# Five query projections in seven products, and smaller moves around them, in a two-layer decoder trunk

## The chip, the cores and the metric

One core of one Trainium2 chip runs the whole kernel. The metric is the device time of one execution in microseconds (us), as the median of several runs. Lower is better. Everything is single precision.

## The reference, cut to what matters

The program is a small decoder trunk. 16 learned rows are put ahead of 512 tokens, so that 528 rows of width 1024 pass through two layers; each layer is a pre-norm branch added to the residual, and a final norm drops the 16 rows. Layer 0 is gated linear attention with 4 heads. Layer 1 is differential attention with 8 heads, and the change is mostly there:

```python
def diff_branch(xn, w_in, lam_vecs, gnorm, w_out, rel_table, lambda_init):
    proj = xn @ w_in                                  # 1024 -> 4 x 2048
    q, k, v, z = jnp.split(proj, 4, axis=-1)
    lam = jnp.exp(jnp.sum(lv[0] * lv[1])) - jnp.exp(jnp.sum(lv[2] * lv[3])) + lambda_init
    ...
    def block(args):                                  # 128 query rows
        s = jnp.einsum('bhpqd,bhpkd->bhpqk', qb, kh) * scale + bias[None, :, None]
        s = jnp.where(dist >= 0, s, -jnp.inf)
        p = jax.nn.softmax(s, axis=-1)                # two maps, p = 0 and 1
        a = p[:, :, 0] - lam * p[:, :, 1]
        return jnp.einsum('bhqk,bhkv->bhqv', a, vh)
    ...
    o = head_rms(o) * gnorm * (1.0 - lambda_init)
    y = jax.nn.silu(z) * o.reshape(B, L, D_INNER)
    return y @ w_out
```

Each head has two query maps and two key maps of width 128, values of width 256 and a gate z of width 256. So q, k, v and z of one head are each a product of the 528 (or the 512 real) normed rows with a 1024 x 256 piece of the weights.

## The kernel before, in words

**Numbers in two parts.** TensorE multiplies float32r operands. To keep precision every operand is split into a high part (a rounded copy, made by ScalarE) and a low part (the difference, made by VectorE) by `split` (L270), and each product is three matmuls: high by high, high by low, low by high. So every weight piece costs one ScalarE and one VectorE instruction before TensorE can use it.

**Two ways to project.** `project` (L414) is the plain one: 8 row blocks of the weights (128 x 128) by three matmuls, 24 matmuls for 128 output columns. For a head's q it runs twice with 512 tokens as the moving operand: 48 matmuls of 512 columns. Its weights come in two parts ("pair"), each a 128 x 1024 split; its result is split straight out of PSUM (L279/L280). A `Unit` (L436) is the other one: the 1024 x 256 piece is cut into 2 x 2 blocks and the rows into two halves of 256 or 264, and seven block products take the place of eight. Each is 12 matmuls (`PASSES`, L42; `product`, L428) of 256 columns where only real tokens are wanted, or of 264. A Unit asks VectorE for four additions of weight blocks (L366), three single splits (a11, a12, a22) and two pair splits (s21, s43); ScalarE copies sums out of PSUM (`partial`, L450, tile u), and four VectorE instructions (L477/L479) put the outputs together. `want_unit` (L356) prepares the weights in the order a11, sums, s21, a12, s43, a22, as far as buffers are free (two pairs, one of each single).

**Units in a chain.** A Unit that is followed by another in the work queue issues the first product of its successor inside its own run (`nxt.first()`, L534), and the successor starts "early". The seven products are p1 to p7 in the code. p1, p6 and p7 gather in one bank of PSUM, bx: after p6 ScalarE copies it (u2), after p7 once more (u3). For an early Unit with no successor, here called lone, the order is p6, p5, p7, p2, p4, p3. Its p7 adds to the bank that u2 is copied from.

**Order of the work.** TensorE's order is the program's order, written out by `Weaver` (L74): a queue of projection work ("filler"), from which `W.fill(us)` issues as much as is asked for, while the attention steps of the current head are put between. VectorE, ScalarE and GpSimd are ordered at build time by priority (`urgent`, `soon`, `at_once`). In layer 1 the loop over heads (L1848) queues, in head hd, the output projection of an earlier pair (`q_diff_out2`, from head 2 on), then z, v, k (Units) and q (plain) of head hd+1. In head 6 the order is k, q, v, z. The key projection may not begin until all scores of the current head are done (`W.stop`, L1868).

**A head's steps** (`diff_steps`, L1675) are A, B, C and E for four blocks of 128 query rows, the longest block (3) first:

- A `scores`: for each map six or twelve matmuls, a VectorE instruction that adds the bias and finds the row's minimum (L1692), an Exp on ScalarE with its sum (L1694). Then VectorE forms the ratio lam x sum0 / sum1 by a reciprocal (L1697) and a small product (L1698), and combines the two maps (L1699).
- B `turn`: transposes of the combined map, and a split (L1707 to L1713).
- C `values`: product with v, a row norm with a power on GpSimd (L1730).
- E `rows`: two transposes of the result (L1737), product with the gate (L1740), and a split.

The list at L1882 gives the order. After each step `W.fill` gets a share of the filler that is left:

```python
        share = {A: 1.5, B: 1.1, C: 1.1, E: 0.5}
        ...
        W.fill(3.0)
        ...
            W.fill(max((W.left - keep) * share[f] / sum(share[g] for g, _ in steps[n:]),
                       ((4.0, 3.0, 5.2, 3.0, 4.6, 3.0, 4.0, 3.0)[hd]) if n == len(steps) - 2 else 2.4 if f is C else 0.0))
```

The last head runs the first six steps so, and the rest in a sequence written out at the end of the kernel, between the parts of the last output projection (L1916 on).

Of the kernel before, what the change touches and what calls it, by code (L numbers as in the profile page):

```python
# [11 lines left out]
F32 = mybir.dt.float32  # L12
# [197 lines left out]
def trunk(ctx, tc, x, meta, g_norm, gla_w_in, gla_w_gate_up, gla_b_gate, gla_gnorm, gla_w_out,  # L210
# [225 lines left out]
    class Unit:  # L436
# [188 lines left out]
    dve.memset(mhalf, -0.5)  # L625
    warm = ps_tile()
# [1035 lines left out]
    def q_diff_q(hd, s):  # L1662
        want_diff(256 * hd)

        def gen():
            for i in range(2):
                bank = pb_tile("bx" if hd else ("bv", "by")[i])
                yield from project(ws.take(), real2, None, NR, [by_halves(bank)])
                assert not hd or heads[hd - 1].scored
                if i == 0:  # L1670
                    s.q = [T(ep, [P, 2, NR], F32R, f"q{j}", bufs=1) for j in range(2)]
                urgent(split)(*[t[:, i, :] for t in s.q], bank, scale=-float(P) ** -0.5)
        return W.add(gen(), 10.3)

    def diff_steps(hd, s, ys):  # L1675
# [3 lines left out]
        def scores(b):  # L1679
# [4 lines left out]
            r.p = []  # L1684
            ko = L - nk
            for m in range(2):
# [8 lines left out]
                r.p.append(p[:, :nk])  # L1695

            dve.reciprocal(st[:, 5:6], st[:, 3:4])  # L1697
            dve.scalar_tensor_tensor(st[:, 5:6], st[:, 5:6], lam, st[:, 2:3], op0=ALU.mult, op1=ALU.mult)  # L1698
# [35 lines left out]
        def rows(r):  # L1734
            pt = ps_tile()
            for m in range(2):
                pe.transpose(pt[:, m * P:(m + 1) * P], r.on[:, m * P:(m + 1) * P], ident)  # L1737
            y = T(ep, [P, 2, P], F32, "yt")
            cs = slice(r.ta, r.ta + P)
            W.mark = dve.tensor_tensor(y, pt[:, :256].rearrange("p (m c) -> p m c", m=2), s.z[:, :, cs], op=ALU.mult)  # L1740
# [7 lines left out]
        return A, lambda b: turn(R[b]), lambda b: values(R[b]), lambda b: rows(R[b])  # L1748
# [99 lines left out]
    for hd in range(D_HEADS):  # L1848
# [24 lines left out]
        if hd == D_HEADS - 2:  # L1873
# [3 lines left out]
            def freed():  # L1877
# [4 lines left out]
        steps = [(A, 0), (A, 1), (B, 0), (A, 2), (C, 0), (B, 1), (E, 0), (A, 3), (C, 1), (B, 2), (E, 1), (C, 2), (B, 3),  # L1882
                 (E, 2), (C, 3), (E, 3)]
# [4 lines left out]
        W.fill(3.0)  # L1888
        for n, (f, b) in enumerate(steps):
# [79 lines left out]
```

## Time and profile before

| what | value |
|---|---|
| median of 3 runs | 971.44 us (970.47 to 972.05) |
| the profiled execution | 970.65 us, its span on the core 968.9 us |
| TensorE clock granted | 0.999 of full speed |
| matmuls | 6993, each with its own weight load |
| VectorE, ScalarE, GpSimd instructions | 1586, 1304, 68 |
| DMA | 104.94 MB, 108 GB/s on average |

In the profile PE is TensorE's matmuls, PEld its weight loads, DVE VectorE, ACT ScalarE, POOL GpSimd, SP the engine that issues most DMAs. A line such as L431 is a line of the kernel; L431 is the matmul of a Unit's products, L421 that of the plain projection, L400 that of everything with both operands in two parts (scores, values, output projection). Matmuls are pipelined, so the shown length of one includes its drain; what one costs in a stream is read from one start to the next.

### The profile page before, as it was taken

Reading aid. Unit: us, or ns where it says so; the run is one execution under the profiler, and the core shown is the slowest. Engines: PE = TensorE matmul, PEld = TensorE weight load, DVE = VectorE, ACT = ScalarE, POOL = GpSimd, SP = SyncE. Lnnn points to the kernel's source line nnn. Section 1 sums busy time; section 2 is a strip of 40 time slices with the busy share of each in tenths; the row PEclk is TensorE's granted clock in tenths of the full one; section 3 lists DMA queues with packets and bytes.
Section 4 is the critical chain, followed back from the end, with each engine's and each line's share of the span. In section 5 each row is a group of like instructions: output and inputs, shape, how many; then the busy total and the mean of one; then the engine's idle time right before and its main releaser. Section 6 shows DMA issues by size and latency. Waiting matters only on the chain.

```text
span 968.9 us, 18048 instructions
## 1 busy us (share of the span) xinstructions
PE 957.2 (99%) x6993; PEld 906.9 (94%) x6993; DVE 778.6 (80%) x1586; ACT 626.8 (65%) x1304; POOL 44.9 (5%) x68
## 2 busy tenths in 40 slices
PE   9999999999999999999999999999999999999997
PEld 8999999999999999998899998998999989989996
DVE  7989885886888787668997987968869769687785
ACT  7776755577647567656757776575675756755583
POOL 1000000000000000000001001000000000000001
PEclk9999999999999999999999999999999999999999
DMA  7322223635363236124355525243342341722212
GB/s 197 88 85 59 82 79 122 147 103 128 116 162 91 85 117 158 53 101 152 99 130 138 143 73 133 75 139 98 99 138 88 118 119 44 182 70 84 89 64 87
DMA packets 128522, 104.94 MB, mean 108 GB/s; under 512 B 51102, under 2 KB 112830, under 8 KB 128433
## 3 DMA queue, kind: packets, MB, share of 16 engines
q1 hardware_dynamic: 123104, 93.80, 35.1%
q10 hardware_dynamic: 5328, 9.95, 2.8%
q8 instruction: 56, 0.92, 0.4%
q14 instruction: 34, 0.27, 0.1%
HBM read 83.64 MB, written 11.80 MB: 99 GB/s over the span
## 4 chain that ended last, share of the span: by engine, by line
PE 88%; ACT 1%; DVE 1%; issue 1%; POOLq 0%; DVEq 0%
PE bx L431 19%; PE bv L431 12%; PE by L431 10%; PE bx L421 10%; PE ps L400 9%; PE bx L972 5%; PE bx L400 3%; PE bv L972 2%; PE by L972 2%; PE ps L1214 2%; PE by L400 2%; PE bv L400 2%; PE ps L1807 1%; PE bx L1807 1%; PE bv L421 1%; PE by L421 1%
## 5 line engine op out<-in xcount | busy, mean ns | idle before, releaser
L277 DVE TENSOR_TENSOR wl<-raw,wh 128x1024 fp32r<-128x1024 f32 x98 | 119.4, 1221 | 23.0 <-ACT wh L276 18.9
L276 ACT ACTIVATE wh<-raw 128x1024 fp32r<-128x1024 f32 x98 | 103.1, 1054 | 48.3 <-PE by L972 22.9
L431 PE MATMUL bv<-x,wh 128*128 128x264 f32 (+1 forms) x656 | 98.6, 287 | 0.0
L431 PE MATMUL bx<-x,wh 128*128 128x264 f32 (+1 forms) x640 | 95.6, 286 | 0.0
L431 PEld LDWEIGHTS bv<-x,wh 128*128 128x128 f32 x656 | 86.8, 189 | 0.6 <-DVE z L479 0.2
L431 PEld LDWEIGHTS bx<-x,wh 128*128 128x128 f32 x640 | 84.6, 188 | 0.7 <-ACT u L452 0.2
L452 ACT ACTIVATE u<-bx 128x264 f32<-128x264 f32 (+1 forms) x120 | 45.3, 379 | 35.5 <-PE bx L431 33.1
L1694 ACT ACTIVATE p<-p,st 128x528 f32<-128x528 f32 (+3 forms) x64 | 36.5, 570 | 41.7 <-DVE st L1692 41.4
L421 PE MATMUL bx<-x,wh 128*128 128x512 f32 (+1 forms) x256 | 62.4, 385 | 0.0
L277 DVE TENSOR_TENSOR wl<-sum,wh 128x1024 fp32r<-128x1024 f32 x41 | 50.1, 1221 | 10.6 <-ACT wh L276 10.5
L431 PE MATMUL bx<-x,wl 128*128 128x264 f32 (+1 forms) x320 | 54.1, 284 | 0.0
L431 PE MATMUL bv<-x,wl 128*128 128x264 f32 (+1 forms) x328 | 53.8, 284 | 0.1
L421 PEld LDWEIGHTS bx<-x,wh 128*128 128x128 f32 x256 | 44.4, 188 | 7.8
L276 ACT ACTIVATE wh<-sum 128x1024 fp32r<-128x1024 f32 x41 | 43.1, 1051 | 9.7 <-PE by L972 3.9
L431 PE MATMUL by<-x,a12h 128*128 128x264 f32 (+1 forms) x320 | 47.5, 286 | 0.1
L1730 POOL TENSOR_TENSOR st<-st,mhalf 128x1 f32<-128x1 f32 x32 | 25.5, 795 | 468.6 <-ACT on L1728 418.2
L431 PE MATMUL bx<-x,a11h 128*128 128x264 f32 (+1 forms) x320 | 46.6, 284 | 0.0
L431 PEld LDWEIGHTS bv<-x,wl 128*128 128x128 f32 x328 | 45.4, 188 | 0.3 <-issue 0.3
L431 PEld LDWEIGHTS bx<-x,wl 128*128 128x128 f32 x320 | 45.3, 188 | 0.3
L431 PEld LDWEIGHTS bx<-x,a11h 128*128 128x128 f32 x320 | 42.4, 188 | 0.6
L431 PEld LDWEIGHTS by<-x,a12h 128*128 128x128 f32 x320 | 42.1, 188 | 0.3 <-ACT t L1658 0.3
L276 ACT ACTIVATE a11h<-raw 128x512 fp32r<-128x512 f32 x41 | 25.7, 626 | 20.7 <-DMA raw<-in_diff_w_in_dram 7.9
(493 smaller groups left out, 2631.9 us busy)
## 6 DMA issues: line engine op xcount, KB each, us to landing
raw<-in_gla_w_in_dram SPq DMA_DIRECT2D x48, 512.0 KB, 4.5
raw<-in_diff_w_in_dram SPq DMA_DIRECT2D x42, 512.0 KB, 4.9
raw<-in_diff_w_in_dram SPq DMA_DIRECT2D x11, 1024.0 KB, 5.9
raw<-in_gla_w_out_dram SPq DMA_DIRECT2D x8, 1024.0 KB, 5.8
raw<-in_diff_w_out_dram SPq DMA_DIRECT2D x8, 1024.0 KB, 6.0
vd<-planes ACTq DMA_DIRECT2D x12, 268.0 KB, 5.8
vd<-keep ACTq DMA_DIRECT2D x12, 264.0 KB, 2.3
T<-bdr SPq DMA_DIRECT2D x8, 264.0 KB, 4.7
```

Source lines behind the costliest of these rows:

```text
L276: act.activation(hi, src, AF.Copy)
L277: dve.tensor_tensor(lo, src, hi.bitcast(F32), op=ALU.subtract)
L400: pe.matmul(ps, l, r, start=first and n == 0, stop=last and n == 2, **kw)
L421: pe.matmul(bank, a[:, k, :], b[k] if n0 is None else b[k][:, n0 + i * nn:n0 + (i + 1) * nn], start=n == 0 and ks[0] == 0, stop=n == len(t ...
L431: pe.matmul(bank[:, :x[q].shape[2]], w[p][:, k * P:(k + 1) * P], x[q][:, k, :], start=first and i == 0, stop=i == len(PASSES) - 1, skip_gr ...
L452: W.moved = act.activation(t, self.bx[:, :self.n], AF.Copy, scale=self.sc)
L972: pe.matmul(banks[i][:, :HT], h.t[p][:, k, mm * P:(mm + 1) * P], s.y[q][k][:, i * HT:(i + 1) * HT], start=n == 0, stop=n == len(PASSES) - 1)
L1214: pe.matmul(o, s.kd[:, i, kc], s.qs[:, i, t0:t0 + n], start=i == 0, stop=i == 1)
L1694: act.activation(p[:, :nk], p[:, :nk], AF.Exp, scale=-1.0, bias=st[:, m:m + 1], accum_out=st[:, 2 + m:3 + m])
L1730: pool.tensor_tensor(ms, ms, mhalf[:, :1], op=ALU.pow)
L1807: pe.matmul(ps[i], yp[hd][p][:, k, b * P:(b + 1) * P], wt[q][cs.start // 512][:, 2 * hd + k, cs.start % 512:(cs.stop - 1) % 512 + 1], star ...
```

## The change

- `q_diff_q`: q of heads 3 to 7 is made by a `Unit` on the 512 real tokens; its two output tiles are then split with the scale already in them. Heads 0, 1 and 2 keep the plain projection. q thereby joins the chain of Units: it follows k early, and in head 6 v follows it.
- A lone Unit writes p7 into a second bank of bx, and the new `third` lets VectorE add u2 to it, where ScalarE copied the sum before.
- The ratio of the two sums is made by three GpSimd instructions; the map with index 1 is scored before the map with index 0.
- `rows` takes two blocks at once (except in the last head): four transposes into one bank, one product with the gate, one split. Two E steps fall out of the list, and yt has one buffer.
- The first fill of a head is 4.0 instead of 3.0; B has at least 2.4 of filler behind it and E at least 1.0.

```diff
+        @at_once
+        def third(self, bank):
+            t = T(up[0], [P, HT], F32, "u", bufs=3)[:, :self.n]
+            if self.sc == 1.0:
+                dve.tensor_tensor(t, bank[:, :self.n], self.u2, op=ALU.add)
+            else:
+                dve.scalar_tensor_tensor(t, bank[:, :self.n], self.sc, self.u2, op0=ALU.mult, op1=ALU.add)
+            return t
...
             def p7():
-                yield from product(self.bx, ws.use(s43)[1], X["t3"], False)
-                self.u3 = self.partial()
+                if early and not nxt:
+                    bank = pb_tile("bx")
+                    yield from product(bank, ws.use(s43)[1], X["t3"])
+                    self.u3 = self.third(bank)
+                else:
+                    yield from product(self.bx, ws.use(s43)[1], X["t3"], False)
+                    self.u3 = self.partial()
                 add(1, 1, self.bv, self.u3, -1)
...
     def q_diff_q(hd, s):
+        scale, qts = -float(P) ** -0.5, []
+
+        def tiles():
+            assert not hd or heads[hd - 1].scored
+            s.q = [T(ep, [P, 2, NR], F32R, f"q{j}", bufs=1) for j in range(2)]
+
+        if hd in (3, 4, 5, 6, 7):
+            def dst():
+                tiles()
+                qts.extend([tok_tile()[:, :NR], tok_tile()[:, :NR]])
+                return qts
+
+            @soon
+            def tail(i):
+                split(*[t[:, i, :] for t in s.q], qts[i])
+
+            return W.add(Unit(want_unit(d_w_in, 256 * hd), Xr, scale, dst, tail), 8.9)
...
-            for m in range(2):
+            for m in (1, 0):
...
-            dve.reciprocal(st[:, 5:6], st[:, 3:4])
-            dve.scalar_tensor_tensor(st[:, 5:6], st[:, 5:6], lam, st[:, 2:3], op0=ALU.mult, op1=ALU.mult)
+            pool.tensor_tensor(st[:, 5:6], st[:, 3:4], minus, op=ALU.pow)
+            pool.tensor_tensor(st[:, 4:5], st[:, 2:3], lam, op=ALU.mult)
+            pool.tensor_tensor(st[:, 5:6], st[:, 5:6], st[:, 4:5], op=ALU.mult)
             dve.scalar_tensor_tensor(r.p[0], r.p[1], st[:, 5:6], r.p[0], op0=ALU.mult, op1=ALU.subtract)
...
         @urgent
-        def rows(r):
+        def rows(*rs):
+            w = P * len(rs)
             pt = ps_tile()
             for m in range(2):
-                pe.transpose(pt[:, m * P:(m + 1) * P], r.on[:, m * P:(m + 1) * P], ident)
-            y = T(ep, [P, 2, P], F32, "yt")
-            cs = slice(r.ta, r.ta + P)
-            W.mark = dve.tensor_tensor(y, pt[:, :256].rearrange("p (m c) -> p m c", m=2), s.z[:, :, cs], op=ALU.mult)
+                for j, r in enumerate(rs):
+                    pe.transpose(pt[:, m * w + j * P:m * w + (j + 1) * P], r.on[:, m * P:(m + 1) * P], ident)
+            y = T(ep, [P, 2, w], F32, "yt", bufs=1)
+            cs = slice(rs[0].ta, rs[0].ta + w)
+            W.mark = dve.tensor_tensor(y, pt[:, :2 * w].rearrange("p (m c) -> p m c", m=2), s.z[:, :, cs], op=ALU.mult)
...
-        steps = [(A, 0), (A, 1), (B, 0), (A, 2), (C, 0), (B, 1), (E, 0), (A, 3), (C, 1), (B, 2), (E, 1), (C, 2), (B, 3),
-                 (E, 2), (C, 3), (E, 3)]
+        steps = [(A, 0), (A, 1), (B, 0), (A, 2), (C, 0), (B, 1), (A, 3), (C, 1), (B, 2), (E, 1), (C, 2), (B, 3),
+                 (C, 3), (E, 3)]
...
-        W.fill(3.0)
+        W.fill(4.0)
...
-                       ((4.0, 3.0, 5.2, 3.0, 4.6, 3.0, 4.0, 3.0)[hd]) if n == len(steps) - 2 else 2.4 if f is C else 0.0))
+                       ((4.0, 3.0, 5.2, 3.0, 4.6, 3.0, 4.0, 3.0)[hd]) if n == len(steps) - 2 else {A: 0.0, B: 2.4, C: 2.4, E: 1.0}[f]))
```

More of the change, by code (lines that the diff above doesn't have):

```diff
@@ L625, in trunk @@
     dve.memset(mhalf, -0.5)
+    minus = cp.tile([P, 1], F32, name="minus")
+    dve.memset(minus, -1.0)
     warm = ps_tile()
@@ L1668, in gen @@
                 yield from project(ws.take(), real2, None, NR, [by_halves(bank)])
-                assert not hd or heads[hd - 1].scored
                 if i == 0:
-                    s.q = [T(ep, [P, 2, NR], F32R, f"q{j}", bufs=1) for j in range(2)]
-                urgent(split)(*[t[:, i, :] for t in s.q], bank, scale=-float(P) ** -0.5)
+                    tiles()
+                urgent(split)(*[t[:, i, :] for t in s.q], bank, scale=scale)
         return W.add(gen(), 10.3)
@@ L1683, in scores @@
             r.st = st = T(ep, [P, 8], F32, "st", bufs=4)
-            r.p = []
+            r.p = [None, None]
             ko = L - nk
-            for m in range(2):
+            for m in (1, 0):
                 p = T(ep, [P, L], F32, "p", bufs=3)
@@ L1746, in A @@
             R[b] = scores(b)
-        return A, lambda b: turn(R[b]), lambda b: values(R[b]), lambda b: rows(R[b])
+        return A, lambda b: turn(R[b]), lambda b: values(R[b]), lambda b: rows(*([R[b]] if hd == D_HEADS - 1 else [R[b], R[b + 1]]))
     def want_last(hd):
```

2 lines of the change are left out of this document (1 added, 1 removed).

## The prediction

> **What bounds the kernel now.** I read the busy times first, then the list of waits with TensorE as the one that waits, then one middle head stretch by stretch, and at last the starts of single matmuls.
>
> ```profile
> PE 957.2 (99%) x6993; PEld 906.9 (94%) x6993; DVE 778.6 (80%) x1586; ACT 626.8 (65%) x1304; POOL 44.9 (5%) x68
> ```
>
> A busy PE need not be a PE at its peak, so this alone settles nothing. The waits do: these are the three longest in total in which TensorE waited for another engine, over 968.9 us.
>
> ```profile
> PE ps L631 <- DVE ones L622: 1.2, 1, 1.2
> PE bx L421 <- DVE wl L277: 0.7, 1, 0.7
> PE ps L1244 <- DVE vm L412: 0.7, 1, 0.7
> ```
>
> None is in a Unit's products (L431), and none above 1.2 us anywhere. TensorE is handed work without a break, and the time is the sum of what its matmuls cost. The windows show the stretches of a middle head (columns: length, then busy PE, PEld, DVE, ACT, POOL): first z, v and k of the next head as Units, then its q by the plain projection, then an output projection with the first scores. The fourth row is a whole head period of 63 us.
>
> ```profile
> 740.30:777.70 37.40, 37.40 (x314) 37.32 (x313) 29.52 (x65) 26.18 (x62) 2.60 (x3) 1.00 0.34 107
> 777.70:789.80 12.10, 12.10 (x59) 9.84 (x58) 6.93 (x14) 6.86 (x15) 0.55 (x1) 1.00 0.61 142
> 789.80:803.50 13.70, 13.70 (x68) 11.61 (x67) 12.41 (x29) 7.07 (x13) 0.00 (x0) 1.00 0.26 78
> ```
>
> ```profile
> 770.00:833.00 63.00, 63.00 (x435) 58.60 (x434) 50.20 (x109) 40.53 (x93) 2.61 (x4) 1.00 0.38 108
> ```
>
> PE fills every one of them at full clock. VectorE has room in the q stretch (6.93 of 12.10 us) and little at the start of a head (12.41 of 13.70, or 91%). So matmul time taken away shortens the run, as long as VectorE still delivers.
>
> **The query projections, matmul side.** What a matmul costs is read from start to start. Here are two products of 256 columns (12 matmuls each, eight by the high and four by the low part), and then a chain of 512-column matmuls of the plain projection (columns: start, length with drain, instruction, count).
>
> ```profile
> 745.89 1.10 PE L431 MATMUL bv<-x,wh 128*128 128x256 f32 x8
> 746.83 0.64 PE L431 MATMUL bv<-x,wl 128*128 128x256 f32 x4
> 747.31 1.10 PE L431 MATMUL bx<-x,wh 128*128 128x256 f32 x8
> 748.25 0.65 PE L431 MATMUL bx<-x,wl 128*128 128x256 f32 x4
> 748.73 0.52 PE L431 MATMUL bx<-x,a11h 128*128 128x264 f32 x3
> ```
>
> ```profile
> 479.08 5.61 PE by L421 x24
> 484.68 5.86 PE bx L421 x48
> ```
>
> From 745.89 to 747.31 and on to 748.73 a product takes 1.42 us, 118 ns for each matmul. From 479.08 to 484.68 the 24 matmuls take 5.60 us, 233 ns for each. One head's q costs 48 x 233 ns = 11.2 us now and seven products of 1.42 us, 9.94 us, after the change. That is 1.23 us less for each head (taking 232.7 ns, since the next inserted step hides a little of the last matmul), and 5 x 1.23 = 6.15 us for heads 3 to 7. It lies wholly on the path, because there PE is the path. Here a page speaks against the change. The Trainium skill, "TensorE: Matmul & The Clock Gate", section Back-to-back issue gap, gives sustained spacings of about 81 ns at 128 columns and 131 ns at 512; by an estimate between its two figures 84 short matmuls would take 8.2 us and 48 long ones 6.3 us, so the seven products would lose. The trace does not agree: its 512-column spacing is 233 ns, and it halves with the columns.
>
> **The same, VectorE's side.** The groups of instructions give the prices (last columns: busy us, mean ns of one, idle before).
>
> ```profile
> L277 DVE TENSOR_TENSOR wl<-raw,wh 128x1024 fp32r<-128x1024 f32 x98 | 119.4, 1221 | 23.0 <-ACT wh L276 18.9 <-PE bx L421 2.9 <-ACT vm L408 0.7
> ...
> L277 DVE TENSOR_TENSOR a11l<-raw,a11h 128x512 fp32r<-128x512 f32 x41 | 28.1, 686 | 12.4 <-ACT a11h L276 12.2
> L366 DVE TENSOR_TENSOR sum<-raw 128x512 f32<-128x512 f32 x41 | 28.1, 686 | 7.0 <-DMA raw<-in_gla_w_in_dram 4.1 <-DMA raw<-in_diff_w_in_dram 2.6
> ...
> L479 DVE TENSOR_TENSOR t<-bv,u 128x264 f32<-128x264 f32 (+1 forms) x33 | 14.0, 425 | 2.9 <-PE bv L431 2.9
> ...
> L1740 DVE TENSOR_TENSOR yt<-ps,z 128x256 f32<-128x256 f32 x32 | 13.4, 418 | 9.6 <-PE ps L1737 9.6
> ...
> L280 DVE SCALAR_TENSOR_TENSOR q<-bx,q 128x512 fp32r<-128x512 f32 x14 | 9.6, 684 | 0.3 <-ACT q L279 0.3
> ...
> L1698 DVE SCALAR_TENSOR_TENSOR st<-st,lam 128x1 f32<-128x1 f32 x32 | 6.9, 216 | 0.6
> ...
> L1697 DVE RECIPROCAL st<-st 128x1 f32<-128x1 f32 x32 | 5.1, 158 | 9.4 <-ACT p L1694 9.4
> ```
>
> The plain q asks VectorE for two pair splits and two result splits: 2 x 1.221 + 2 x 0.684 = 3.81 us. The Unit asks for four block additions, three single splits, two pair splits, four output instructions and two result splits: 4 x 0.686 + 3 x 0.686 + 2 x 1.221 + 4 x 0.425 + 2 x 0.684 = 10.31 us. That is 6.50 us more for each head, at most, since neighbours overlap by some tens of ns. ScalarE gets the same three single splits and two or three bank copies; at 65% busy it has the room. I cost both at nothing as long as they hide under the matmuls. From 740.30 to 789.80 VectorE is busy 29.52 + 6.93 = 36.45 of 49.50 us. The new sum stays below the 48.3 us that PE then needs, even with all of it put there (43.0 us).
>
> **The third product of a lone Unit.** The sum after p7 moves from ScalarE to VectorE, at 425 ns by the row of its like (L479), and p7 no longer waits for the copy of u2. No such wait is among TensorE's waits above, so nothing is gained where it is made now (k of most heads); below nothing it can hardly go, since one VectorE instruction takes the place of one on ScalarE, and both are ahead of the same next one. In the heads that change, the lone Unit is q instead of k: 0.43 us more for VectorE. I take 0 for the time. Without cover, each use would cost its 0.43 us.
>
> **The ratio on GpSimd, and the order of the maps.** Off VectorE go 0.158 + 0.216 us for each block, 1.50 us for each head of four blocks. On GpSimd come three instructions; two of them follow the second sum, since the power needs only the map that is now first. The nearest row is the power of the row norm:
>
> ```profile
> L1730 POOL TENSOR_TENSOR st<-st,mhalf 128x1 f32<-128x1 f32 x32 | 25.5, 795 | 468.6 <-ACT on L1728 418.2 <-DVE wl L277 30.1 <-DVE p L1699 13.2
> ```
>
> So two instructions cost between 0.32 us (if as quick as VectorE's 158 ns) and 1.59 us, against 0.37 us now: the combination of the maps (L1699) comes -0.05 to +1.22 us later. I take +1.2, the like row. L1699 waits in VectorE's queue, and a weight split of 1.22 us may stand behind it, which a Unit waits for; but a split made that much later is still ahead of its product while VectorE has a tenth of its time free. The one who needs the combined map is step B. It has the least room in the last head:
>
> ```profile
> 915.92 0.77 DVE L1699 SCALAR_TENSOR_TENSOR p<-p,st,p 128x528 f32<-128x528 f32 x1
> ```
>
> ```profile
> 919.80 0.60 PE L1707 MATMUL ps<-ident,p 128*128 128x128 f32 x4
> ```
>
> Ready at 916.69, used at 919.80: 3.1 us of cover for 1.2. The time is unchanged. Without that cover it would be 1.2 us for each of 32 blocks. GpSimd's only other work there is the power of step C, which could queue behind a ratio for the same 1.2 us; the filler behind C covers it.
>
> **Rows in pairs, and the fills.** Four transposes stay four transposes for TensorE: no gain. VectorE's four products of 256 columns at 0.418 us and as many split halves of that size become two and two of 512 at 0.684 us (the L280 row): 3.34 us become 2.74, 0.60 less a head. The first block of a pair waits for the second, and its reader is an output projection of a later head. The fills move PE work about and add none. The first one does not even move it where output projections are the filler: they come in steps of 1.4 us (L1784), and 3.0 and 4.0 both take three steps. Cost 0.
>
> **The sum.** TensorE: -6.15 us. VectorE for each changed head: +6.50 + 0.43 - 1.50 - 0.60 = +4.83, so 55.0 of 61.8 us, 89% where it is 80% now. I add 0.2 us of new waits for each of the five heads, 1.0 us in all, taken from the lower part of the first rival's span. The profiled execution took 970.65 us (its span 968.9), 0.8 under the median of 971.44. It should become 965.5, and the median 971.44 - 6.15 + 1.0 = **966.3 us**.
>
> **The rivals.** First, and on the other side: q comes late to the first scores. The rows show q's end before, at the same place of this head.
>
> ```profile
> 789.77 0.40 PE L400 MATMUL bx<-wh,y 128*128 128x512 f32 x1
> ...
> 793.99 1.61 PE L400 MATMUL ps<-k,q 128*128 128x264 f32 x12
> ```
>
> ```profile
> 792.70 0.58 ACT L279 ACTIVATE q<-bx 128x512 fp32r<-128x512 f32 x1
> ...
> 793.67 0.68 DVE L280 SCALAR_TENSOR_TENSOR q<-bx,q 128x512 fp32r<-128x512 f32 x1
> ```
>
> The last matmul of q ends at about 789.77; its ScalarE half starts only at 792.70, 2.9 us later, behind other work, and the low half is done at 794.35, 4.6 us after the end. The scores begin at 793.99, and those of the second map half of 1.46 us later, at 794.72: 0.4 us of room. Afterwards the chain has one VectorE instruction more (an output sum of 0.43 us), at a lower priority. What speaks for room is that the map that is ready first (its outputs are finished one product, 1.42 us, earlier) is scored first, so that the late one has 4.95 us. If the chain grows by 0.43 to 5.0 us, the wait is nothing to 0.1; with one more place in a queue (1.22 us) it is 1.3 us. Up to 0.6 us a head the result stays below 969.5; between 0.9 and 1.23 us for each head nearly all is eaten, about 970 to 971.4. It decides at 1.23 us. If two links of the chain each wait the 2.9 us seen here, the chain is 2 x 2.9 + 0.43 + 0.58 + 0.68 = 7.5 us and the wait 2.5 us a head: 5 x (2.5 - 1.23) = 6.4 us lost, 978 us.
>
> Second: VectorE's new work isn't hidden because it comes in one place. q's pair s43 can be split only when k has given back its own pair, at k's end; q's p7 follows two products (2.84 us) after that. In these come the block addition, the pair split, two output sums and the splits of k: 0.69 + 1.22 + 0.85 + 1.37 = 4.13 us. What is over, 1.3 us, less the time of the first eight matmuls of p7, 0.94 us, is 0.35 us for each head: 967.0 us, with 1.75 us of waits where the sum has 1.0. Against it stands that k is in the same place behind v now, and none of TensorE's waits lies there.
>
> Third: the loads of the weights set the pace, not the columns.
>
> ```profile
> L431 PEld LDWEIGHTS bv<-x,wh 128*128 128x128 f32 x656 | 86.8, 189 | 0.6 <-DVE z L479 0.2
> ```
>
> If each of 84 loads cost its 189 ns, q would take 15.9 us instead of 11.2, +4.7 a head, 995 us. The 118 ns spacing in a stretch where PEld is as full as PE (37.32 of 37.40) says that loads overlap. This is also the way in which the page's spacings above would have it.
>
> Fourth: the change does not do what it says, for a Unit that is not chained (then nothing of the third product applies) or a bank that is not free. The second is the nearer one: p7 takes the second bx, which the Unit before has left long ago. Price 0, and the sum stays.
>
> **How the numbers follow.** About 0.2%, 2 us, is what a measurement of this kernel can tell from no change. Chances: the sum as forecast, waits under 0.6 us a head, with the second rival's size among them, 0.68; the first rival with 0.6 to 1.23 us, 0.17, of which a third is still faster by 2 us; its slower form, 0.11; weight loads, 0.01; a shift elsewhere that returns the gain, 0.03. So faster 0.74, within 0.2% 0.14, slower 0.12. The range reaches from all of the 6.15 us and the waits of today that might go (two of 0.7 us), with the spread of the runs below, 963.1, to the end of the first rival where all is eaten, 971.5; that leaves out its slower form and little else.
>
> **What would show it.** Right: L421 falls by 240 matmuls and L431 rises by 420; a head period of about 61.8 us; VectorE near 89% in a middle head; no wait of TensorE above 0.5 us in heads 2 to 6. Wrong in the first way: waits of scores (L400, ps<-k,q) on the q tile at a head's start. In the second: waits of L431 on the pair split. In the third: starts of q's products more than 130 ns apart. A gain well over 7 us would mean that TensorE's stream had gaps that its waits don't show.

## The result, and the profile after

| | before | after |
|---|---|---|
| median, same chip | 971.19 us (6 runs, 970.47 to 972.05) | 977.01 us (6 runs, 976.63 to 978.37) |
| ratio, 95% interval | | 1.0061 [1.0049, 1.0073]: 0.6% slower |
| profiled execution, its span | 970.65, 968.9 us | 976.72, 974.9 us |

Predicted were 966.3 us. The page's busy times, by engine:

```profile
PE 954.6 (98%) x7173; PEld 912.2 (94%) x7173; DVE 799.6 (82%) x1561; ACT 633.1 (65%) x1309; POOL 83.0 (9%) x164
```

TensorE has 180 matmuls more (240 long ones gone, 420 short ones come), as it should, and they cost what was forecast. A product of q and the start of the next, in the timeline of TensorE:

```profile
722.87 1.10 PE L431 MATMUL bx<-x,wh 128*128 128x256 f32 x8
723.81 0.65 PE L431 MATMUL bx<-x,wl 128*128 128x256 f32 x4
724.29 1.11 PE L431 MATMUL by<-x,a12h 128*128 128x256 f32 x8
```

From 722.87 to 724.29 it is 1.42 us again. So the matmul side gave its 6.15 us. The span grew by 974.9 - 968.9 = 6.0 us all the same, which means that about 12.1 us of waiting came in. The list of TensorE's waits holds 8.4 us of it: it comes to 12.7 us in all, where it came to 4.3 before. It counts a wait only from the end that the profile gives the matmul before it. Read from one start to the next, with the drain of that matmul, the listed places lose 10.6 us more than before, and gaps too short for the list lose the rest (each spacing taken against the median of its shape in the kernel before). From the list (engine and line waited for: us in total, times, longest):

```profile
PE bx L431 <- ACT u L452: 3.7, 4, 1.4
PE ps L1260 <- ACT vm L408: 1.4, 1, 1.4
...
PE by L431 <- DVE t L486: 0.7, 2, 0.3
```

The first line is new: a Unit's product waits until ScalarE has copied the bank that it adds to. The wait at L1260, in the first layer, was 0.7 us before. Of the others about half are new, on ScalarE and VectorE, and none of the new ones is longer than 0.6 us.

Three head periods of the kernel after, from the first scores of one head to those of the next (length, then busy PE, PEld, DVE, ACT, POOL):

```profile
669.28:733.16 63.88, 62.68 (x472) 59.97 (x471) 55.99 (x113) 42.65 (x96) 7.63 (x16) 1.00 0.36 107
733.16:795.50 62.34, 62.17 (x472) 59.86 (x471) 53.22 (x106) 41.95 (x95) 7.75 (x16) 1.00 0.37 109
795.50:859.18 63.68, 62.24 (x471) 59.87 (x470) 54.41 (x109) 42.09 (x95) 7.22 (x16) 1.00 0.38 109
```

The middle one is nearly the forecast 61.8 us. The others are 1.5 and 1.3 us longer, with VectorE busy for 88% and 85% of the time, where the middle one has 85% too. So a share of busy time doesn't tell where it is lost; the places do. ScalarE and TensorE around 809 us:

```profile
808.53 1.06 ACT L276 ACTIVATE wh<-raw 128x1024 fp32r<-128x1024 f32 x1 [1.24 <-DVE raw L366]
809.49 0.37 ACT L452 ACTIVATE u<-bx 128x256 f32<-128x256 f32 x1
```

```profile
809.91 0.97 PE L431 MATMUL bx<-x,wh 128*128 128x256 f32 x6 [1.44 <-ACT u L452]
```

The copy takes 0.37 us and its bank was long full, but ScalarE works in order: a weight split stands ahead of it, and that one waits 1.24 us for a block addition on VectorE. At 911 us it is a split that waits for a DMA:

```profile
910.34 0.63 ACT L276 ACTIVATE a11h<-raw 128x512 fp32r<-128x512 f32 x1 [4.70 <-DMA raw<-in_diff_w_in_dram]
910.88 0.37 ACT L452 ACTIVATE u<-bx 128x264 f32<-128x264 f32 x1
```

```profile
911.30 1.24 PE L431 MATMUL bx<-x,wh 128*128 128x264 f32 x8 [1.35 <-ACT u L452]
```

The Trainium skill, "TensorE: Matmul & The Clock Gate", table of specifications, calls the queues of ScalarE, VectorE and GpSimd strictly first in, first out; these rows of ScalarE agree.

### The profile page after: what moved, and what is told of

It is laid out like the page before. It is cut to its first block, busy times and chain, and to the rows that moved or that the text cites. A ratio compares the mean times of both kernels' runs of the same rounds, so it can differ in the third digit from the quotient of the medians.

```text
span 974.9 us, 18485 instructions
## 1 busy us (share of the span) xinstructions
PE 954.6 (98%) x7173; PEld 912.2 (94%) x7173; DVE 799.6 (82%) x1561; ACT 633.1 (65%) x1309; POOL 83.0 (9%) x164
## 4 chain that ended last, share of the span: by engine, by line
PE 73%; DVE 7%; ACT 5%; DMA 3%; issue 2%; POOL 1%; SPq 0%; POOLq 0%; ACTq 0%; DVEq 0%
PE bx L431 18%; PE bv L431 10%; PE by L431 10%; PE ps L400 7%; PE bx L988 5%; PE bx L421 4%; DMA raw<-in_diff_w_in_dram 3%; PE by L988 2%; PE bv L988 2%; PE ps L1230 2%; PE bx L400 2%; DVE wl L277 1%; ACT p L1726 1%; PE ps L1842 1%; PE bx L1842 1%
## 5 line engine op out<-in xcount | busy, mean ns | idle before, releaser
L431 PE MATMUL bv<-x,wh 128*128 128x264 f32 (+1 forms) x736 | 109.5, 286 | 0.2
L431 PE MATMUL bx<-x,wh 128*128 128x264 f32 (+1 forms) x720 | 105.7, 285 | 3.7 <-ACT u L452 3.7
L431 PEld LDWEIGHTS bx<-x,wh 128*128 128x128 f32 x720 | 94.4, 188 | 5.1 <-ACT u L452 4.7
L431 PEld LDWEIGHTS bv<-x,wh 128*128 128x128 f32 x736 | 96.8, 188 | 1.0 <-DVE t L486 0.3
L277 DVE TENSOR_TENSOR wl<-sum,wh 128x1024 fp32r<-128x1024 f32 x46 | 56.2, 1222 | 12.2 <-ACT wh L276 12.0
L431 PE MATMUL bv<-x,wl 128*128 128x264 f32 (+1 forms) x368 | 61.2, 285 | 0.1
L431 PE MATMUL bx<-x,a11h 128*128 128x264 f32 (+1 forms) x360 | 53.8, 285 | 0.0
L277 DVE TENSOR_TENSOR a11l<-raw,a11h 128x512 fp32r<-128x512 f32 x46 | 31.6, 687 | 17.2 <-ACT a11h L276 17.0
L1729 POOL TENSOR_TENSOR st<-st,minus 128x1 f32<-128x1 f32 x32 | 20.9, 653 | 283.7 <-ACT p L1726 231.5
L556 POOL TENSOR_TENSOR st<-st,mhalf 128x1 f32<-128x1 f32 (+1 forms) x20 | 11.8, 588 | 388.6 <-DVE st L555 388.6
```

What stands on the lines that cost most here:

```text
L277: dve.tensor_tensor(lo, src, hi.bitcast(F32), op=ALU.subtract)
L431: pe.matmul(bank[:, :x[q].shape[2]], w[p][:, k * P:(k + 1) * P], x[q][:, k, :], start=first and i == 0, stop=i == len(PASSES) - 1, skip_gr ...
L556: pool.tensor_tensor(dst, dst, mhalf[:np_, :dst.shape[1]], op=ALU.pow)
L1729: pool.tensor_tensor(st[:, 5:6], st[:, 3:4], minus, op=ALU.pow)
```

## The experiments

Every time below is a median, beside the kernel before on the same chip (970.4 to 970.6 us), with the ratio's 95% interval.

| run | kernel | us | ratio |
|---|---|---|---|
| e1_only_q | before, q of heads 3 to 7 as Units | 970.29 | 0.9998 [0.9989, 1.0007] |
| e2_no_q | after, all q plain | 975.01 | 1.0044 [1.0031, 1.0058] |
| e3_no_third | after, without `third` | 973.36 | 1.0031 [1.0019, 1.0043] |
| e4_ratio_dve | after, ratio on VectorE | 972.12 | 1.0016 [1.0007, 1.0025] |
| e5_no_third_ratio_dve | both of these | 968.80 | 0.9984 [0.9975, 0.9993] |
| e6_third_alone | before, `third` | 974.00 | 1.0031 [1.0019, 1.0044] |
| e7_ratio_alone | before, GpSimd ratio and map order | 974.08 | 1.0036 [1.0023, 1.0048] |
| e8_pairs_fills_alone | before, rows in pairs and fills | 973.38 | 1.0028 [1.0017, 1.0039] |
| e9_ratio_unhurried | e7, combination out of the urgent step | 974.81 | 1.0045 [1.0032, 1.0058] |
| e10_e5_q3to6 | e5, q of head 7 plain | 968.52 | 0.9983 [0.9974, 0.9992] |
| e11_q3to6_order | before, q of heads 3 to 6, map order | 970.15 | 0.9993 [0.9984, 1.0001] |
| e12_q3to6_order_pairs | e11, rows in pairs | 974.34 | 1.0035 [1.0020, 1.0049] |
| e13_order_alone | before, map order | 971.47 | 1.0013 [1.0005, 1.0022] |
| e15_ratio_behind_copy | e7, Exp behind the copy of u | 970.94 | 1.0004 [0.9995, 1.0013] |
| e16_q3to6_ratio_behind_copy | e18, ratio on GpSimd | 971.80 | 1.0013 [1.0004, 1.0022] |
| e17_third_second_layer | before, `third` in the second layer | 972.38 | 1.0024 [1.0013, 1.0035] |
| e18_q3to6_behind_copy | e10, Exp behind the copy of u | 967.94 | 0.9973 [0.9963, 0.9983] |
| e19_fills_alone | before, fills | 973.59 | 1.0036 [1.0023, 1.0050] |

**The query Units against the rest.** Theory A: the q Units themselves bring the waits, through the copies of u on ScalarE. Theory B: the parts beside q do. e1 puts only the new `q_diff_q` into the kernel before, e2 takes only that out of the kernel after:

```diff
-        if hd in (3, 4, 5, 6, 7):
+        if hd in ():
```

> Kernel before with one part of the change alone: q of heads 3 to 7 as a Unit (7 products). Theory A (the Units of q themselves: their weight preparation and output work fills VectorE and ScalarE, copies of u wait in ScalarE's queue behind work that waits for VectorE or a transfer, and TensorE waits for the copies, some 10 us over the second layer): 974 to 977 us, slower than before. Theory B (the parts beside q cost the time, q saves its 6.15 us): 965 to 967 us.

> Kernel after with q of all heads by the plain projection again, everything else as after. Theory A: 971 to 973.5 us (what is left is the 1.7 us that the first layer lost with the third product on VectorE). Theory B: 976 to 983 us.

Neither holds alone. Without q the kernel is 4.6 us slower than before, so the parts that were costed at nothing carry most of the loss (B). But q alone gains nothing either: its span is 968.9 us as before's, so 6.15 us of matmul time went into as much waiting. Both times lie between what the two theories gave. Of e1's waiting the list holds 3.7 us (8.1 in all, 4.3 before): only 0.8 us on u, and as much on the gate product of a rows step:

```profile
PE bx L431 <- ACT u L452: 0.8, 1, 0.8
PE ps L400 <- DVE yt L1756: 0.8, 1, 0.8
```

The rest is spread over several places. At the start of head 3 the forecast's first rival can be seen, in TensorE's timeline and then in VectorE's:

```profile
666.51 0.50 PE L400 MATMUL bv<-wh,hT 128*128 128x512 f32 x1 [0.50 <-DVE t L481]
...
668.84 0.64 PE L400 MATMUL ps<-k,q 128*128 128x264 f32 x3 [0.44 <-DVE q L277]
```

```profile
666.04 0.41 DVE L481 SCALAR_TENSOR_TENSOR t<-bv,u 128x256 f32<-128x256 f32 x1
666.37 0.68 DVE L277 TENSOR_TENSOR q<-t,q 128x512 fp32r<-128x512 f32 x1
666.97 1.22 DVE L277 TENSOR_TENSOR wl<-raw,wh 128x1024 fp32r<-128x1024 f32 x1
668.11 0.68 DVE L277 TENSOR_TENSOR q<-t,q 128x512 fp32r<-128x512 f32 x1
```

The second split of q stands behind one weight split of 1.22 us, "one more place in a queue" as the rival put it, and the scores wait 0.44 us for it. An output projection waits 0.50 us as well, for the bank that q's last sum has yet to leave.

**Part by part.** Theory C: each part has a price of its own and they add. Theory D: they compete for the same room. e3 and e4 take one part out of the kernel after, e5 both; e6, e7 and e8 put one part alone into the kernel before. For `third`:

```diff
-                if early and not nxt:
+                if False:
```

> Kernel after, but p7 of every Unit adds to the bank of p6 again and ScalarE copies it (no third). Theory A: between 974.5 and 979 us: the first layer gets its 1.7 us back, a lone q may lose some of that by waiting for the copy of u2. Theory B with the third product as the culprit: 968 to 973 us.

> Kernel after, but the ratio of the sums by two VectorE instructions again; second map still first. Theory A: 976 to 979 us, no gain, as the ratio on GpSimd only takes work off VectorE. Theory B with the GpSimd chain as the culprit (32 blocks whose combined map comes later and holds VectorE's queue): 968 to 973 us.

> Kernel after without the third product in another bank and with the ratio on VectorE again, both at once. Theory C (each part has a price of its own and the prices add): 977.0 - 3.6 - 4.9 = 968.5 us, faster than before. Theory D (both took room from the same waits in the last heads, so undoing one is as good as undoing both): 971.5 to 972.5 us.

> Kernel before with the third product of lone Units in another bank alone (VectorE adds, where ScalarE copied). Theory C: 971.7 to 973 us, 1.3 to 2.6 us slower than before, most of it in the first layer, where TensorE waits for the tile kd at 260 us and for vm at 389 us. Theory D: within 0.5 us of before, as VectorE has room without the new q.

> Kernel before with the ratio on GpSimd and the second map's scores first, alone. Theory C: 971.5 to 974 us, the waits of VectorE for the ratio come back as waits of TensorE in the last two heads. Theory D: within 0.7 us of before.

> Kernel before with rows in pairs, the shorter list of steps and the new fills, alone. Theory C: 970.4 to 971.5 us, next to nothing: the part of the 4.6 us that the third product and the ratio leave. Theory D: within 0.5 us of before.

Each part that the forecast costed at nothing makes the kernel before some 3 us slower by itself: `third` 974.00 - 970.63 = 3.4, the ratio 3.5, pairs and fills 2.8. With q's -0.1 that sums to 9.6, where the whole change costs 5.8, so C does not hold as a sum. D, which expected at most 0.7 us of each, does not hold either, and for pairs and fills both theories missed. Taken out of the kernel after (e3 lies between the times of A and B, e4 where B put it), `third` brings 3.6, the ratio 4.9, both 8.2 us by the medians. By the ratios it is 2.9, 4.4 and 7.5, since the kernel after was measured beside 971.2 us and these runs beside 970.4 to 970.6. In this direction the two prices nearly add, as C had it (968.5). With both out, e5 is faster than before.

**The ratio on GpSimd.** Theory E: VectorE waits in its queue for GpSimd, so an Exp waits for VectorE, the copy of u waits behind the Exp, and TensorE waits for the copy. Theory F: it is the later combination that costs. e9 moves the combination (L1702 in e7) out of the urgent step, so that VectorE needn't hurry to it:

```diff
-            dve.scalar_tensor_tensor(r.p[0], r.p[1], st[:, 5:6], r.p[0], op0=ALU.mult, op1=ALU.subtract)
             return r
...
-            R[b] = scores(b)
+            r = R[b] = scores(b)
+            dve.scalar_tensor_tensor(r.p[0], r.p[1], r.st[:, 5:6], r.p[0], op0=ALU.mult, op1=ALU.subtract)
```

> The ratio on GpSimd and the second map first, alone on the kernel before, and the combination of the two maps taken out of the urgent step, so that VectorE's queue is ordered with other work ahead of it. Theory E (VectorE waits in its queue for GpSimd's ratio, ScalarE's Exp waits for VectorE, the copy of u behind the Exp waits too, and TensorE waits for the copy): 970.5 to 972 us, most of the 3.4 us are back, and the waits of L431 on u in heads 3 to 6 fall under 1.5 us. Theory F (GpSimd's ratio costs by its later combination of the maps, not by the queue): 974 us or more, as the combination now comes later still.

That was a miss for E: 974.81, no better than e7, as F had it. Setting the instruction streams of e7 and of the kernel before side by side tells why. TensorE's is the same throughout. ScalarE's differs in four places, one in each of four heads, and each time in one pair of neighbours:

```diff
 ACTIVATE a12h<-raw 128x512
-ACTIVATE u<-bx 128x256
-ACTIVATE p,st<-p,st 128x272
+ACTIVATE p,st<-p,st 128x272
+ACTIVATE u<-bx 128x256
 ACTIVATE p,st<-p,st 128x272
```

e9 has the same four. The order on ScalarE is settled at build, and with GpSimd's instructions in the program it came out with the Exp of block 1 first. What that does can be seen in one head, in ScalarE's timeline of the kernel before and of e7, with TensorE's product of e7 at the end:

```profile
809.22 0.38 ACT L452 ACTIVATE u<-bx 128x256 f32<-128x256 f32 x1 [1.45 <-PE bx L431]
811.48 0.53 ACT L1694 ACTIVATE p<-p,st 128x272 f32<-128x272 f32 x1 [1.88 <-DVE st L1692]
```

```profile
813.05 0.52 ACT L1696 ACTIVATE p<-p,st 128x272 f32<-128x272 f32 x1 [3.29 <-DVE st L1694]
...
813.57 0.36 ACT L452 ACTIVATE u<-bx 128x256 f32<-128x256 f32 x1
```

```profile
813.98 1.21 PE L431 MATMUL bx<-x,wh 128*128 128x256 f32 x8 [1.40 <-ACT u L452]
```

In both, ScalarE stands idle and waits. Before, it waits for the bank of u and copies at once; in e7 it waits for VectorE's minimum, with the copy that TensorE needs behind it. This is theory G: the price is the four places and not GpSimd. e15 undoes just these. Where the scores of block 1 are issued inside a product that ends in a copy of u (W.copying), the Exps are issued after that copy:

```diff
+            hold = W.copying and b == 1
...
+                if not hold:
+                    act.activation(p[:, :nk], p[:, :nk], AF.Exp, scale=-1.0, bias=st[:, m:m + 1], accum_out=st[:, 2 + m:3 + m])
...
+            def finish(ins):
+                for m in (1, 0) if hold else ():
+                    with tc.issue_after(ins) if ins else ExitStack():
+                        act.activation(r.p[m], r.p[m], AF.Exp, scale=-1.0, bias=st[:, m:m + 1], accum_out=st[:, 2 + m:3 + m])
```

ScalarE's and TensorE's orders are then those of the kernel before, instruction by instruction, and VectorE's and GpSimd's those of e7. e13 has the other half of e7 by itself, the order of the maps.

> The kernel before with the second map's scores first, and nothing else; the ratio stays on VectorE. TensorE's and ScalarE's orders stay those of the kernel before, instruction by instruction; VectorE's order shifts at a few places by one. Theory G (the price of e7 lies in four places at which ScalarE's order has an Exp ahead of the copy of u): no change, 970.4, within 1 us. Rival (the map order itself is what costs): 973 to 974.

> e7 (ratio on GpSimd, second map first), with the two Exps of block 1 put behind the copy of u where the scores lie inside a product that ends in such a copy: so ScalarE's and TensorE's orders are again those of the kernel before, and VectorE's and GpSimd's those of e7. Theory G: all of the price goes, 970.5, between 969.7 and 971.3, and TensorE's four waits on u in heads 3 to 6 (0.32, 0.36, 0.82, 1.57 us in e7) are gone. Theories E and F (GpSimd's latency, through VectorE's queue or the later combination): 973.5 to 974.5, as e7.

e15 takes 970.94 us, and the interval of its ratio holds 1. All of the 3.5 us are gone but 0.4. Yet VectorE waits for GpSimd as before; its waits, first of e7 and then of e15:

```profile
DVE p L1702 <- POOL st L1701: 23.2, 30, 2.3
```

```profile
DVE p L1723 <- POOL st L1722: 22.6, 30, 2.3
```

And the head of TensorE's list, first of e7 and then of e15:

```profile
PE bx L431 <- ACT u L452: 2.4, 4, 1.4
```

```profile
PE ps L647 <- DVE ones L636: 1.1, 1, 1.1
PE bx L426 <- DVE wl L282: 0.8, 1, 0.8
```

No wait on u is left in e15's list. So E falls in its first link, and F falls: 22.6 us of VectorE's waiting for GpSimd cost next to nothing, while four pairs of neighbours in the wrong order cost 3.1 us. What E had right is the rest of its chain, an Exp ahead of the copy. The map order alone was expected to cost nothing, within 1 us, and costs 0.9 us; its one new wait in the second layer (0.8 us in the last head) is on the same tile as that of `third`, next.

**Where `third` costs.** e17 has it in the second layer only:

```diff
+                if early and not nxt and len(heads) == D_HEADS:
```

> The kernel before with the third product in another bank in the second layer's lone Units only (in e6 it is there in the first layer's four as well, and took 974.0, 3.0 us over the kernel before). By the waits of e6's trace, 2.1 us lie in the first layer and 1.5 us in the last head: about 971.9, between 971.2 and 972.6. Rival (the price comes from the later heads' lone Units wherever they are): 973.5 to 974. Rival (it is the first layer alone): 970.5.

It takes 972.38 us, 1.8 over before, as read from e6's waits; the other half of e6's price thus lies in the first layer, which no run takes apart. TensorE's instructions are the same in e17 as before, and matmul by matmul e17 falls behind at one place of the second layer, in the last head, by 1.2 us, the difference of the two spans (970.1 and 968.9). GpSimd, ScalarE and VectorE there, first in the kernel before, then in e17 with TensorE:

```profile
933.08 0.71 POOL L1730 TENSOR_TENSOR st<-st,mhalf 128x1 f32<-128x1 f32 x1 [30.59 <-ACT on L1728]
...
933.83 0.47 ACT L1731 ACTIVATE on<-ps,st 128x256 f32<-128x256 f32 x1 [0.35 <-POOL st L1730]
...
936.80 0.69 DVE L1566 SCALAR_TENSOR_TENSOR z<-z,t 128x512 f32<-128x512 f32 x1 [0.55 <-ACT t L1565]
...
937.52 0.28 DVE L410 TENSOR_TENSOR am<-ps,am 32x128 fp32r<-32x128 f32 x1
```

```profile
933.87 1.22 DVE L277 TENSOR_TENSOR x<-raw,x 128x1024 fp32r<-128x1024 f32 x1
933.90 1.60 POOL L1744 TENSOR_TENSOR st<-st,mhalf 128x1 f32<-128x1 f32 x1 [31.51 <-ACT on L1742]
...
935.53 0.47 ACT L1745 ACTIVATE on<-ps,st 128x256 f32<-128x256 f32 x1 [1.25 <-POOL st L1744]
...
938.31 0.69 DVE L1580 SCALAR_TENSOR_TENSOR z<-z,t 128x512 f32<-128x512 f32 x1 [0.50 <-ACT t L1579]
939.03 0.28 DVE L410 TENSOR_TENSOR am<-ps,am 32x128 fp32r<-32x128 f32 x1
...
939.37 0.56 PE L400 MATMUL ps<-k,q 128*128 128x144 f32 x3 [0.95 <-DVE am L410]
```

The small split `am` frees a bank that scores need. In both kernels it stands behind the same gate product, which waits for ScalarE about as long (0.55 and 0.50 us). The difference lies farther back. GpSimd's power of the row norm starts 0.8 us later in e17 and takes 1.60 us instead of 0.71: it starts when a split of VectorE has just begun (933.87) and ends 0.41 us behind that split's end. ScalarE waits for the power, and what stands behind it comes later. e6 and e13 show the same 1.60 us and the same wait on `am` in the last head. An instruction of 0.42 us did not cost its 0.42 us in each of the lone Units; in the second layer its price stands at this one place. That the place can be mended was not tried.

**Pairs or fills.** e19 is the kernel before with the fills alone:

```diff
-        W.fill(3.0)
+        W.fill(4.0)
...
-                       ... if n == len(steps) - 2 else 2.4 if f is C else 0.0))
+                       ... if n == len(steps) - 2 else {A: 0.0, B: 2.4, C: 2.4, E: 1.0}[f]))
```

> The kernel before with the new fills (first 4.0 where it was 3.0, and at least 1.0 after each E), rows one by one as before. e8, with the fills and the rows in pairs, took 2.8 us more than the kernel before. If the fills move the work into the waits: 972.5 to 973.5. If the pairs do: 970.4 to 971. If each has a part of it: about 971.8.

The fills alone cost as much as both together (973.59 against e8's 973.38). But the waits are not the same. Half of e19's price is one wait at the end, where the gate product of a rows step is late; there GpSimd's power takes 2.05 us, and ScalarE waits 2.21 us for it. From the list of TensorE's waits:

```profile
PE ps L400 <- DVE yt L1740: 1.7, 2, 1.5
```

e8's list lacks this wait and has 1.2 us on sums of VectorE and 0.5 us on u instead. So the fills cost, and that the pairs cost nothing is not shown by the two times alone.

**Towards a better kernel.** In e5 most of the waits left in the second half of the run lie where q of head 7 is made (904 to 918 us). e10 leaves that q plain, `if hd in (3, 4, 5, 6):`. e11 and e12 build up from the kernel before with that q: the map order, then the rows in pairs with the old fills.

> Kernel after without third and with the ratio on VectorE, q as a Unit in heads 3 to 6 only (head 7 plain). If the waits of 904 to 925 us come from the longer chain k, q, v, z in head 6: 968.8 + 1.2 - 2.5 = 967.5 us. If they come from pairs and fills: 969.5 us or more.

> Kernel before with q of heads 3 to 6 as a Unit and the second map's scores first, nothing else. Saves 4 x 1.23 = 4.9 us of matmuls. If the order of the maps removes the two waits of scores and output banks at a head's start that q alone had (1.3 us in the first head) and the last heads are free of waits as in before: 967 to 968.5 us. If VectorE's share alone decides: 969.5 to 971 us.

> As the run with q of heads 3 to 6 and the order of the maps, and rows in pairs with the shorter list of steps; old fills. If the 2.7 us of pairs and fills alone come from the fills: 0.5 us faster than without pairs (0.6 us less VectorE work a head). If they come from the pairs: 1 to 3 us slower than without.

e10 is as fast as e5 with 1.2 us less taken off TensorE; it lies between its two expectations. e11 differs from e10 by the pairs and the fills alone and is 1.6 us slower, so the two together, which cost 2.8 us in the kernel before, do no harm beside the query Units. e12 gives no price of the pairs: its runs lie between 970.0 and 977.7 us, and its profile shows a single long GpSimd instruction (below). e16 and e18 take e10 and put the Exps of block 1 behind the copy as in e15; e16 has the ratio on GpSimd, e18 on VectorE.

> The kernel after without the third product in another bank, q as Units in heads 3 to 6 only, the ratio on GpSimd, and block 1's Exps behind the copy of u as in e15. Its neighbour is e10, which has the ratio on VectorE and took 968.5. Theory G: the ratio on GpSimd is free once the order is mended, 968.5, between 967.5 and 969.5. Theories E and F: e10's time and the 3.5 us of e7, 971 to 972. Theory D (the parts use the same room): between, about 970.

> e10 (the kernel after without the third product, the ratio on VectorE, q as Units in heads 3 to 6; 968.5) with block 1's Exps behind the copy of u: two neighbouring instructions of ScalarE change places once, in head 5, nothing else on TensorE, VectorE or ScalarE. Theory G: the 0.33 us wait on u of that place goes, 968.2, between 967.5 and 968.6. Rival (the wait only moves): 968.5.

e18 is the best version: 967.94 us, ratio 0.9973, 2.5 us below the kernel before. The turned pair took away the wait it was meant for (0.2 us in e10's list); matmul by matmul e18 gains 0.6 us there, between 804 and 809 us, and the medians of e10 and e18 differ by 0.6. TensorE has no wait on u any more; the head of its list:

```profile
PE bx L747 <- DVE y L727: 1.8, 3, 0.8
PE bv L436 <- DVE t L498: 1.8, 2, 1.2
```

e16 was a miss for theory G: the ratio on GpSimd, free in e15, costs 971.80 - 967.94 = 3.9 us beside the query Units. No wait on u is in its list. Its longest line, 1.8 us on a sum of VectorE, stands in e18's list too; new is:

```profile
PE by L436 <- DVE t L498: 0.7, 1, 0.7
```

TensorE's instructions are the same in both, and matmul by matmul e16 falls behind mainly at six places, at 768, 791, 803, 829, 893 and 926 to 930 us of its trace, by 0.2 to 1.0 us each. ScalarE's order is the same between 700 and 916 us, so most of the loss comes from no turned pair on ScalarE. VectorE's order differs at many places, and VectorE waits 16.7 us in all for the ratio, once 1.45 us at 921 us. So it may be VectorE's order, or GpSimd's latency now that VectorE has less room. The runs do not tell these apart; it stays open, and with it whether the price of the ratio in the kernel after is the one that e15 takes back.

## Why the prediction was wrong, point by point

- **TensorE, -6.15 us: right.** The 118 ns spacing held, and it was right to go by the trace's spacing. The chances for late weight loads and for a change that doesn't do what it says could have stayed where they were.
- **The step that failed: the new waits, put at nothing but for 1.0 us.** In its words, "I cost both at nothing as long as they hide under the matmuls", "I take 0 for the time", "The time is unchanged", "Cost 0", and the one term that was left, "0.2 us of new waits for each of the five heads, 1.0 us in all". About 12.1 us came. In the kernel before, one at a time, q's other work ate its 6.15 us, `third` cost 3.4, the ratio 3.5 and the fills 3.1 us. The sums behind the zeros were sound: VectorE was forecast at 89% of a head and shows 85 to 88%. But what was compared was amounts of work, and the wait comes from where the work stands: a copy of 0.37 us behind an Exp or a split that waits, a power of one column that meets a split and holds up ScalarE. e15 shows the first by itself, in the kernel before: same work, same engines, one pair of neighbours turned in four heads, 3.1 us. For `third` and the fills the traces show a place each; for the rest of the 12.1 us, and for the ratio beside the query Units, the cause stays open.
- **"I take 0 for the time" (third): wrong, 3.4 us alone.** "Both are ahead of the same next one" looked only at the Unit. In the last head, as e17's trace shows it, a power on GpSimd met a split and everything behind it came later. And it was costed for the heads that change, while 4 of the 11 lone Units are in the first layer, where half of the price lay.
- **"The time is unchanged" (ratio): wrong, 3.5 us alone, though its latency was overrated.** GpSimd's products take 0.2 to 0.4 us in the mean, not 0.8:

```profile
L1730 POOL TENSOR_TENSOR st<-st,lam 128x1 f32<-128x1 f32 x32 | 11.7, 366 | 10.5 <-ACT p L1726 10.0
L1731 POOL TENSOR_TENSOR st<-st 128x1 f32<-128x1 f32 x32 | 7.0, 219 | 2.5
```

- **"Cost 0" (pairs, fills): wrong for the fills,** 3.1 us alone. That 3.0 and 4.0 take the same three steps speaks for the first fill of some heads only: in e19 the order of TensorE's instructions differs from the kernel before's in most heads. For the pairs no run settles it: e8 takes no longer than e19, and e12 is spread over 7.6 us.
- **The first rival** was right as a mechanism where q is alone (e1, 0.44 us at one head start). In the kernel after, with the map order turned, no scores wait for q. Its slower form gave 978 us, and 977.0 came, but by other waits; the number agrees and the reason does not.
- **The second rival** put the cost at VectorE's pair split; no product of a Unit waits for one in the list of waits of the kernel after. Its kind, work that comes in one place, was nearer to the truth than its place.
- **What would show it:** "no wait of TensorE above 0.5 us in heads 2 to 6" was the right thing to look at, and 1.44 us at 809.9 us refuted it.

## What to carry to other kernels

Where one engine is full and the others feed it through queues whose order is settled at build, a share of 85% says nothing about waits: for each instruction that the full engine waits for, look at what stands ahead of it in its queue and what that one waits for. Before a part is costed at nothing, expect some microseconds from a shuffled order, try each part alone, and set the two instruction streams side by side; a pair of neighbours that changed places can be put back by a rule of issue, which in the kernel before was worth 3.1 us, half of the gain on the full engine. Small instructions on GpSimd that others wait for deserve the same look: in these traces a power of 0.55 us took 1.6 us and more where it met splits on VectorE. And a gain on the full engine is kept only as far as the order around it is mended: of 4.9 us (four heads), e18 keeps 2.5.

## What was not expected of the hardware

GpSimd's power of a single column, 0.56 us in the median of the kernel before and at most 2.27, took 3.23 us once in e12 (540 us), and ScalarE, which scales the values by it, and TensorE behind it waited:

```profile
539.87 3.23 POOL L1746 TENSOR_TENSOR st<-st,mhalf 128x1 f32<-128x1 f32 x1 [9.72 <-ACT on L1744]
...
540.26 1.22 DVE L277 TENSOR_TENSOR wl<-raw,wh 128x1024 fp32r<-128x1024 f32 x1
541.40 0.69 DVE L366 TENSOR_TENSOR raw<-raw,sum 128x512 f32<-128x512 f32 x1
...
542.00 0.69 DVE L277 TENSOR_TENSOR a22l<-raw,a22h 128x512 fp32r<-128x512 f32 x1
543.13 0.47 ACT L1747 ACTIVATE on<-ps,st 128x256 f32<-128x256 f32 x1 [3.34 <-POOL st L1746]
...
543.83 0.71 PE L400 MATMUL ps<-v,aT 128*128 128x256 f32 x3 [2.02 <-ACT aT L276]
```

VectorE runs splits and block additions without a break until 542.69, and the power ends at 543.10, 0.41 us later. The traces of the 20 kernels agree. Of GpSimd's instructions on a single column, 924 overlap no TENSOR_TENSOR of VectorE with both inputs in SBUF, and none of these takes more than 0.73 us. All 278 that take more than 0.9 us overlap one, and 262 of them end 0.37 to 0.45 us behind the end of one. The powers of 1.60 and 2.05 us in the last head, above, are among them. No run moves such a pair apart, so this is a regularity of the traces and not an experiment.

After these 2.02 us without a matmul the granted clock (the column behind POOL) fell to half and stayed there for 3.4 us:

```profile
540.00:543.83 3.83, 1.80 (x9) 1.13 (x7) 2.71 (x6) 0.70 (x3) 3.10 (x1) 1.00 0.25 61
544.40:547.82 3.42, 3.40 (x9) 2.69 (x9) 2.47 (x4) 2.37 (x6) 0.55 (x1) 0.50 0.50 174
547.82:551.00 3.18, 3.18 (x15) 2.55 (x15) 1.44 (x3) 0.83 (x1) 0.00 (x0) 1.00 0.01 3
```

Half of 3.42 us is 1.7 us, so a wait of 2 us cost almost as much again. The Trainium skill, "TensorE: Matmul & The Clock Gate", Part 1 on the clock gate, tells of a fall to half the clock after an idle window of about 3.4 us; the half agrees, and here 2.02 us without a matmul were enough. e12's twelve executions go by the clock: three with a mean of 0.999 took 970.0 to 971.7 us, seven with 0.997 or less 974.1 to 977.7. The median of e12 is therefore not read as the price of the pairs.
